# RMS norms of a decoder layer: mean square by float32r products with a constant matrix, inverse root by Ln, Exp and one Newton step

## The chip, the core and the metric

The kernel runs on one core of one Trainium2 chip. The core has five engines that run side by side, each working through its own instructions in order: TensorE (PE) for matrix products, VectorE (DVE) for elementwise work, ScalarE (ACT) for activations and casts, GpSimd (POOL) and SyncE (SP), which here mostly issues the transfers (DMAs) between memory and SBUF. Products land in PSUM, eight banks of 128 x 512 float32. The metric is the device time of one execution in microseconds.

## The reference

One hybrid decoder layer on 1024 tokens of width 1024, float32: a SwiGLU half step (FFN1), a mixer of three branches (RWKV-7, sliding-window attention, cross-attention into 256 memory tokens) merged by gates and one output projection, and a second SwiGLU half step (FFN2). Each of the three has an RMS norm on its input and one on its output, which is then added to the residual stream; the memory tokens have a norm of their own.

```python
def rms_norm(x, g):
    xf = x.astype(jnp.float32)
    y = xf * lax.rsqrt(jnp.mean(xf * xf, axis=-1, keepdims=True) + NORM_EPS)
    return (y * g.astype(jnp.float32)).astype(x.dtype)

f1 = swiglu(rms_norm(h, ffn1_pre_g[l]), ffn1_w_in[l], ffn1_w_out[l])
h = h + HALF_STEP * rms_norm(f1, ffn1_post_g[l])
u = rms_norm(h, mix_pre_g[l])
...
h = h + rms_norm(merged @ w_out[l], mix_post_g[l])
f2 = swiglu(rms_norm(h, ffn2_pre_g[l]), ffn2_w_in[l], ffn2_w_out[l])
h = h + HALF_STEP * rms_norm(f2, ffn2_post_g[l])
```

## The kernel before

**Layout.** Features lie on the partitions and tokens along the free axis: an activation is eight tiles (`KD`) of 128 features by 512 tokens for each of the two halves of the tokens (`HALVES`). A norm thus sums over the partitions and over the eight tiles, and its result, one number for each token, is wanted on all partitions.

**Products.** Every large product is made from three float32r matmuls (`mm3`, lines 330 to 332): an operand is split into a high part, rounded to float32r by ACT, and a low part, the rest, by DVE (`operand`, lines 264 and 266, for weights; `split`, lines 393 and 394, for activations). Weights come as strips into five raw buffers and are split ahead of their use into eight operand buffers (`prefetch`). The two FFN products are computed by a scheme that replaces eight block products by seven and forms sums and differences of blocks on DVE (`factors_part`, `factors_end`, `out_sums`, `out_forms`, `ffn_out_sum`). In an FFN, the first 9 (FFN1) or 13 (FFN2) gates are computed from the first half's factors while the second half's are still being made.

**A norm.** ACT squares the eight tiles and DVE adds them up into one tile `sq` (`sum_squares`, lines 403 and 407; the squares have three buffers of a ring in the pool of the stage). `rstd` does the rest. For each block of 128 tokens, `sq` is the stationary operand of a float32 matmul and a column of ones the moving one, which puts the sum of a token on one partition: `ps_ms`, 128 x 4 for 512 tokens (line 365). On that small tile DVE makes the mean (line 370), a first guess of the inverse root by an integer shift, and three Newton steps (lines 375 to 381). The norms of the layer's last output (`quick`) take a reciprocal on DVE, Sqrt on ACT (line 373) and one Newton step instead. Then four more float32 matmuls, with the column of a block repeated as the stationary operand and the identity as the moving one, spread the result over all partitions: `ps_rs`, 128 x 512 in PSUM (line 387). A float32 matmul stands in the profile as two instructions. The scaling of the eight tiles by gain and root is one DVE instruction each (lines 419, 447 and 730), reading `ps_rs`.

**Where the norms stand.** `factors_norm` normalizes the input of FFN1 (half 0 in `start`, half 1 in `ffn_in`) and of FFN2 (halves 0 and 1); `post_norm` normalizes the output of FFN1, of the mixer's projection and of FFN2, adds the residual (line 733) and, at the end, stores the result; `pre_norm` normalizes the mixer's input. The last output's second half is done in two parts of 256 tokens (`TAIL`). The memory norm calls `rstd` for its columns. With the memory norm there are fourteen.

**Order.** The order of the instructions on each engine is set by a planner, which simulates the engines and takes what is ready, by priority; `high_priority` moves work ahead, and `keep_in_program_order` pins an instruction behind the one traced before it on its engine. Where a norm gets a `between`, its matmuls are pinned, and the function is traced between the two groups of matmuls, so that PE works on other products while the root is made: at the start (`while_x`), and in the last output's norms, where a part of the last product (`more`, `ffn_out`) stands there. Elsewhere the planner places them.

**ACT's tables.** Ln, Exp, Silu, Tanh, Sqrt and Sin each need a table on ACT, and a load (`ACT_TABLE_LOAD`) stands in front of an instruction whose function isn't in the table that is loaded.

Of the kernel before, what the change touches and what calls it, by code (L numbers as in the profile page):

```python
# [24 lines left out]
MEM = 256  # L25
EPS = 1e-6
# [72 lines left out]
class WindowBlock(Block):  # L99
# [108 lines left out]
class Builder:  # L208
# [146 lines left out]

    def rstd(self, sqs, width, pool, n=TH, columns=False, quick=False, between=None):
        nc = self.nc
        V = nc.vector  # L360
        nb = n // P
        ps = self.psum("ps_ms")
        for j in range(nb):
            for i, sq in enumerate(sqs):
                mm = nc.tensor.matmul(ps[:, j : j + 1], sq[:, j * P : (j + 1) * P], self.ones, start=i == 0, stop=i == len(sqs) - 1)
                if between:
                    self.tc.keep_in_program_order(mm)
        m, y, hm, q = (pool.tile([P, 4], F32, tag="rs" + t, name="rs" + t, bufs=2)[:, :nb] for t in "myhq")
        with self.tc.high_priority(offset=self.lead):
            V.tensor_scalar(m, ps[:, :nb], 1.0 / width, EPS, ALU.mult, ALU.add)  # L370
            if quick:
                V.reciprocal(y, m)
                nc.scalar.activation(y, y, ACT.Sqrt)
            else:
                V.tensor_scalar(y.bitcast(I32), m.bitcast(I32), 1, None, ALU.logical_shift_right)
                V.tensor_scalar(y.bitcast(I32), y.bitcast(I32), -1, 0x5F3759DF, ALU.mult, ALU.add)
            V.tensor_scalar(hm, m, -0.5, None, ALU.mult)
            for _ in range(1 if quick else 3):
                V.tensor_tensor(q, y, y, ALU.mult)
                V.tensor_tensor(q, q, hm, ALU.mult)  # L380
                V.scalar_tensor_tensor(y, q, 1.5, y, ALU.add, ALU.mult)
        if between:
            between()
        out = self.psum("ps_rs")
        with self.tc.high_priority(offset=self.lead):
            for j in range(nb):
                mm = nc.tensor.matmul(out[:, j * P : (j + 1) * P], y[:, j : j + 1].broadcast_to([P, P]), self.ident, start=True, stop=True)
                if between:
                    self.tc.keep_in_program_order(mm)
        return (out, y) if columns else out  # L390

    def split(self, x, hi, lo):
        self.nc.scalar.copy(hi, x)  # L393
# [2 lines left out]
    def sum_squares(self, xs, pool):  # L396

        nc = self.nc
        n = xs[0].shape[1]
        acc = None  # L400
        for x in xs:
            sq = pool.tile([P, n], F32, tag=f"sq{n}", name="sq", bufs=3)
            nc.scalar.activation(sq, x, ACT.Square)
            if acc is None:
                acc = sq
            else:
                nc.vector.tensor_tensor(acc, acc, sq, ALU.add)
        return acc

    def pre_norm(self, x, part, gname, u, pool):  # L410

        h, lo, hi = part
        xs = [t[h][:, lo:hi] for t in x]
        rs = self.rstd([self.sum_squares(xs, pool)], D, pool, hi - lo)[:, : hi - lo]
        for k in range(KD):
            if lo == 0:
                u[k][h] = self.u_tile(), self.u_tile()
            t = pool.tile([P, TH], F32, tag="un", name="un", bufs=2)[:, : hi - lo]
            self.nc.vector.scalar_tensor_tensor(t, xs[k], self.vec(gname, k), rs, ALU.mult, ALU.mult)
            self.split(t, *(y[:, lo:hi] for y in u[k][h]))  # L420
# [20 lines left out]
    def factors_norm(self, xs, part, gname, pool, between=None, then=None):  # L441

        h, lo, hi = part
        xs = [x[h][:, lo:hi] for x in xs]
        rs = self.rstd([self.sum_squares(xs, pool)], D, pool, hi - lo, between=between)[:, : hi - lo]
        for k in range(KD) if then else (0, 4, 1, 5, 2, 6, 3, 7):
            self.nc.vector.scalar_tensor_tensor(xs[k], xs[k], self.vec(gname, k), rs, ALU.mult, ALU.mult)
            if then:
                then(k)
# [269 lines left out]
    def post_norm(self, acc, part, gcol, xr, pool, save=None):  # L719

        nc = self.nc
        h, lo, hi = part
        cols = slice(h * TH + lo, h * TH + hi)
        xs = [acc[k][h][:, lo:hi] for k in range(KD)]
        end = save is self.io["out"]
        with self.tc.high_priority(offset=self.urgent if end else 0):
            sq = self.sum_squares(xs[KH:] + xs[:KH] if h else xs, pool)
        rs = self.rstd([sq], D, pool, hi - lo, quick=end, between=self.between if end else None)[:, : hi - lo]
        for k in range(KD):
            nc.vector.scalar_tensor_tensor(xs[k], xs[k], gcol(k), rs, ALU.mult, ALU.mult)  # L730

            e = nc.gpsimd if end and cols.stop == T and k in (0, 2, 4) else nc.vector
            e.tensor_tensor(xs[k], xs[k], xr[k], ALU.add)
            if save is not None:
                nc.sync.dma_start(save[:, k, cols], xs[k])
# [451 lines left out]
    def start(self, x, pool, km_d, vm_d):  # L1187
        nc, tc, io = self.nc, self.tc, self.io
        V = nc.vector
        keep = tc.keep_in_program_order  # L1190
        send = self.send = lambda *a: keep(nc.sync.dma_start(*a))
        mm = lambda *a, start, stop: keep(nc.tensor.matmul(*a, start=start, stop=stop))
# [64 lines left out]
        sqs = mem_squares()  # L1257
# [19 lines left out]
        for i in (0, 1):  # L1277
            t = pool.tile([P, 512], F32, tag="mkv", name="vm", bufs=3)
# [249 lines left out]
    def build(self):  # L1528
        nc, tc, io = self.nc, self.tc, self.io
        with contextlib.ExitStack() as outer, tc.tile_pool(reuse_waits="tile", name="consts", bufs=1) as cp, \  # L1530
# [27 lines left out]
            with quarters() as self.qpool:  # L1558
                x = self.acc_tiles()
# [110 lines left out]
```

## Time and profile before

| | |
|---|---|
| median of 3 runs | 2318.09 us (2318.04 to 2320.25) |
| profiled execution | 2322.86 us, span 2321.1 us |
| PE busy | 2278.9 us, 98% of the span |
| DVE busy | 1653.6 us, 71% |
| ACT busy | 962.3 us, 41% |
| POOL busy | 95.7 us, 4% |
| granted TensorE clock, mean | 0.997 |

The span runs from the first to the last instruction; the profiled execution's own time is 1.8 us longer. A matmul row's duration overlaps with the next one's, so that what a matmul costs PE is read from the starts of its neighbours, not from its duration. Rows of a timeline give start, length, engine, line, operation, output and inputs, shapes and count; in brackets stands the idle time before it and who ended it. PEld is a weight load.

### The profile page before, as it was taken

The numbers are of one execution on the slowest core, as the hardware profiler recorded it, in microseconds if no ns is written. First come the engines' busy times: TensorE is split into PE (matmuls) and PEld (weight loads), VectorE is DVE, ScalarE is ACT, GpSimd is POOL, SyncE is SP. The second block draws the span as 40 slices with busy tenths as digits, with TensorE's granted clock in tenths as the row PEclk, the third lists the DMA queues.
The fourth block names the chain that finished last, engine by engine and source line by source line (L and its number), as shares of the span: only waits on it lengthen the run. The fifth ranks groups of instructions, "written<-read, shape, count | busy, mean of one in ns | idle before, by whom it ended". The sixth has DMA issues, their size and how long they took to land. (4 is left out here: it accounts for less than half of the span.)

```text
span 2321.1 us, 33883 instructions
## 1 busy us (share of the span) xinstructions
PE 2278.9 (98%) x12080; PEld 1862.7 (80%) x12080; DVE 1653.6 (71%) x2790; ACT 962.3 (41%) x1791; POOL 95.7 (4%) x134
## 2 busy tenths in 40 slices
PE   8999999999999999999999999999999999999998
PEld 6778888888888777888878888778888778888887
DVE  6998666666688786895645466565899886666666
ACT  5522333454445544223444455234552223345451
POOL 0000000000000000001310000241000000000000
PEclk9999999999999999999999999999999999999999
DMA  8577545586644446325435425555467775558663
GB/s 276 160 251 255 171 158 166 171 289 207 190 160 144 111 118 186 131 96 183 139 130 179 129 95 170 173 178 160 158 212 229 263 243 172 168 182 271 214 195 114
DMA packets 280778, 417.70 MB, mean 180 GB/s; under 512 B 82304, under 2 KB 104320, under 8 KB 280352
## 3 DMA queue, kind: packets, MB, share of 16 engines
q1 hardware_dynamic: 231552, 388.20, 51.9%
q10 hardware_dynamic: 49056, 27.34, 4.2%
q8 instruction: 95, 1.56, 0.3%
q14 instruction: 75, 0.61, 0.1%
HBM read 284.89 MB, written 129.50 MB: 179 GB/s over the span
## 5 line engine op out<-in xcount | busy, mean ns | idle before, releaser
L264 ACT CAST w_hi<-w_raw 128x512 fp32r<-128x512 f32 x594 | 366.2, 620 | 774.8 <-PE px L331 140.9
L266 DVE TENSOR_TENSOR w_lo<-w_raw,w_hi 128x512 fp32r<-128x512 f32 x594 | 415.4, 702 | 218.0 <-ACT w_hi L264 181.1
L330 PE MATMUL po<-u,w_hi 128*128 128x512 f32 (+1 forms) x476 | 181.8, 382 | 0.0
L332 PE MATMUL po<-u,w_lo 128*128 128x512 f32 (+1 forms) x476 | 181.1, 380 | 0.0
L331 PE MATMUL po<-u,w_hi 128*128 128x512 f32 (+1 forms) x476 | 181.0, 380 | 0.0
L330 PE MATMUL pgate<-u,w_hi 128*128 128x512 f32 x384 | 155.2, 404 | 0.0
L332 PE MATMUL pgate<-u,w_lo 128*128 128x512 f32 x384 | 151.5, 394 | 0.0
L331 PE MATMUL pgate<-u,w_hi 128*128 128x512 f32 x384 | 149.7, 390 | 0.0
L330 PE MATMUL px<-f,w_hi 128*128 128x512 f32 x352 | 139.0, 395 | 6.4 <-DVE up L600 3.9
L330 PE MATMUL px<-u,w_hi 128*128 128x512 f32 x352 | 137.5, 391 | 3.0 <-ACT w_hi L264 2.1
L331 PE MATMUL pz<-u,w_hi 128*128 128x512 f32 x352 | 137.3, 390 | 0.6 <-DVE u L394 0.6
L331 PE MATMUL px<-f,w_hi 128*128 128x512 f32 x352 | 137.6, 391 | 0.0
L330 PE MATMUL pz<-u,w_hi 128*128 128x512 f32 x352 | 137.3, 390 | 0.3 <-DVE m L587 0.3
L332 PE MATMUL px<-f,w_lo 128*128 128x512 f32 x352 | 137.5, 391 | 0.0
L331 PE MATMUL px<-u,w_hi 128*128 128x512 f32 x352 | 137.0, 389 | 0.0
L332 PE MATMUL pz<-u,w_lo 128*128 128x512 f32 x352 | 137.0, 389 | 0.0
L332 PE MATMUL px<-u,w_lo 128*128 128x512 f32 x352 | 137.0, 389 | 0.0
L394 DVE TENSOR_TENSOR u<-hid,u 128x512 fp32r<-128x512 f32 x114 | 78.5, 689 | 49.2 <-ACT u L393 46.6
L331 PEld LDWEIGHTS po<-u,w_hi 128*128 128x128 f32 x476 | 89.5, 188 | 17.3
L332 PEld LDWEIGHTS po<-u,w_lo 128*128 128x128 f32 x476 | 89.5, 188 | 17.3
L330 PEld LDWEIGHTS po<-u,w_hi 128*128 128x128 f32 x476 | 89.5, 188 | 17.2
L393 ACT CAST u<-hid 128x512 fp32r<-128x512 f32 x114 | 70.7, 620 | 69.6 <-DMA hid<-form_d 61.8
(347 smaller groups left out, 5127.6 us busy)
## 6 DMA issues: line engine op xcount, KB each, us to landing
w_raw<-in_ffn_in SPq DMA_DIRECT2D x220, 256.0 KB
hid<-form_d SPq DMA_DIRECT2D x154, 256.0 KB
w_raw<-in_win SPq DMA_DIRECT2D x112, 256.0 KB
ws<-in_ffn_out SPq DMA_DIRECT2D x88, 256.0 KB
form_d<-g SPq DMA_DIRECT2D x88, 256.0 KB
ffn_sum_d<-ws SPq DMA_DIRECT2D x88, 256.0 KB
w_raw<-ffn_sum_d SPq DMA_DIRECT2D x88, 256.0 KB
form_d<-h SPq DMA_DIRECT2D x66, 256.0 KB
```

Source lines behind the costliest of these rows:

```text
L264: self.nc.scalar.copy(hi, x)
L266: self.nc.vector.tensor_tensor(lo, x, hi.bitcast(F32), ALU.subtract)
L330: mm(out, wh, xh, start=first, stop=False, **kw)
L331: mm(out, wh, xl, start=False, stop=False, **kw)
L332: mm(out, wl, xh, start=False, stop=last, **kw)
L393: self.nc.scalar.copy(hi, x)
L394: self.nc.vector.tensor_tensor(lo, x, hi.bitcast(F32), ALU.subtract)
```

## The change

All norms but the memory norm take a new function, `inverse_root`. ACT copies the sum of squares, with a small constant added that stands for epsilon, into a float32r tile (`sq_hi`), and DVE makes the rest (`sq_lo`). Two float32r matmuls with a constant 128 x 128 matrix of 1/1024 as the stationary operand put the mean on all partitions, 128 x 512 in PSUM. ACT takes Ln of it, then Exp with a scale of -0.5, and squares that; two DVE instructions make one Newton step over the full width. The result lies in SBUF; the scalings read it there. The table that has both Ln and Exp is asked for right behind the high part. All ACT instructions of the function but none of DVE's are pinned in the traced order, the two matmuls only where there is a `between`; the function `between` is traced behind all of it. The high part, the low part and the root share the ring of the squares, which has four buffers in place of three. Two constant tiles are set at the start. `rstd` keeps one form, for the memory norm.

```diff
-    def rstd(self, sqs, width, pool, n=TH, columns=False, quick=False, between=None):
+    def rstd(self, sqs, width, pool, n, between):
...
-            if quick:
-                V.reciprocal(y, m)
-                nc.scalar.activation(y, y, ACT.Sqrt)
...
+    def inverse_root(self, sq, pool, between=None):
+
+        nc = self.nc
+        n = sq.shape[1]
+        hi, lo, y = (pool.tile([P, n], t, tag=f"sq{n}", name=name, bufs=4) for t, name in ((F32R, "sq_hi"), (F32R, "sq_lo"), (F32, "rs")))
+        ps = self.psum("ps_rs")[:, :n]
+        V, S = nc.vector, nc.scalar
+        keep = self.tc.keep_in_program_order
+        with self.tc.high_priority(offset=self.lead):
+            keep(S.activation(hi, sq, ACT.Identity, bias=self.eps))
+            V.scalar_tensor_tensor(lo, sq, self.eps, hi.bitcast(F32), ALU.add, ALU.subtract)
+            keep(S.preload_act_table_set("natural_log_exp_and_others"))
+            for i, x in enumerate((hi, lo)):
+                mm = nc.tensor.matmul(ps, self.mean_r, x, start=i == 0, stop=i == 1)
+                if between:
+                    keep(mm)
+            keep(S.activation(y, ps, ACT.Ln))
+            keep(S.activation(y, y, ACT.Exp, scale=-0.5))
+            keep(S.activation(sq, y, ACT.Square))
+            V.scalar_tensor_tensor(sq, ps, -0.5, sq, ALU.mult, ALU.mult)
+            V.scalar_tensor_tensor(y, sq, 1.5, y, ALU.add, ALU.mult)
+        if between:
+            between()
+        return y
...
-            sq = pool.tile([P, n], F32, tag=f"sq{n}", name="sq", bufs=3)
+            sq = pool.tile([P, n], F32, tag=f"sq{n}", name="sq", bufs=4)
...
-        rs = self.rstd([self.sum_squares(xs, pool)], D, pool, hi - lo)[:, : hi - lo]
+        rs = self.inverse_root(self.sum_squares(xs, pool), pool)
...
-        rs = self.rstd([self.sum_squares(xs, pool)], D, pool, hi - lo, between=between)[:, : hi - lo]
+        rs = self.inverse_root(self.sum_squares(xs, pool), pool, between)
...
-        rs = self.rstd([sq], D, pool, hi - lo, quick=end, between=self.between if end else None)[:, : hi - lo]
+        rs = self.inverse_root(sq, pool, self.between if end else None)
...
-        ps, col = self.rstd(sqs, D, pool, MEM, True, between=while_mem)
+        ps, col = self.rstd(sqs, D, pool, MEM, while_mem)
...
+            self.mean_r = cp.tile([P, P], F32R, name="mean_r")
+            nc.vector.memset(self.mean_r.bitcast(F32), 1.0 / D)
+            self.eps = cp.tile([P, 1], F32, name="eps")
+            nc.vector.memset(self.eps, EPS * D / P)
```

More of the change, by code (lines that the diff above doesn't have):

```diff
@@ L364, in rstd @@
             for i, sq in enumerate(sqs):
-                mm = nc.tensor.matmul(ps[:, j : j + 1], sq[:, j * P : (j + 1) * P], self.ones, start=i == 0, stop=i == len(sqs) - 1)
-                if between:
-                    self.tc.keep_in_program_order(mm)
+                keep(nc.tensor.matmul(ps[:, j : j + 1], sq[:, j * P : (j + 1) * P], self.ones, start=i == 0, stop=i == len(sqs) - 1))
         m, y, hm, q = (pool.tile([P, 4], F32, tag="rs" + t, name="rs" + t, bufs=2)[:, :nb] for t in "myhq")
@@ L381, in rstd @@
                 V.scalar_tensor_tensor(y, q, 1.5, y, ALU.add, ALU.mult)
-        if between:
-            between()
+        between()
         out = self.psum("ps_rs")
@@ L386, in rstd @@
             for j in range(nb):
-                mm = nc.tensor.matmul(out[:, j * P : (j + 1) * P], y[:, j : j + 1].broadcast_to([P, P]), self.ident, start=True, stop=True)
-                if between:
-                    self.tc.keep_in_program_order(mm)
-        return (out, y) if columns else out
+                keep(nc.tensor.matmul(out[:, j * P : (j + 1) * P], y[:, j : j + 1].broadcast_to([P, P]), self.ident, start=True, stop=True))
+        return out, y
+    def inverse_root(self, sq, pool, between=None):
[4 more added lines that the diff above has]
+        V, S = nc.vector, nc.scalar
+        keep = self.tc.keep_in_program_order
+        with self.tc.high_priority(offset=self.lead):
[4 more added lines that the diff above has]
+                mm = nc.tensor.matmul(ps, self.mean_r, x, start=i == 0, stop=i == 1)
+                if between:
+                    keep(mm)
[5 more added lines that the diff above has]
+        if between:
+            between()
+        return y
     def split(self, x, hi, lo):
```

7 lines of the change are left out of this document (3 added, 4 removed).

## The prediction

> **What bounds the kernel now.** I read the page first (engines and slices), then the table by stage, the groups by line, and the timeline at each norm. The columns of the stage rows are the stretch, its length, then busy time of PE, weight loads, DVE, ACT and POOL, granted clock, DMA share, GB/s.
>
> ```profile
> PE 2278.9 (98%) x12080; PEld 1862.7 (80%) x12080; DVE 1653.6 (71%) x2790; ACT 962.3 (41%) x1791; POOL 95.7 (4%) x134
> ...
> 40.00:100.00 60.00, 57.37 (x255) 45.90 (x254) 50.07 (x93) 33.56 (x59) 0.00 (x0) 1.00 0.58 188
> 1700.00:1900.00 200.00, 195.47 (x853) 158.25 (x852) 182.38 (x299) 65.71 (x116) 0.00 (x0) 1.00 0.72 237
> ...
> 1805.07 0.47 PE L330 MATMUL px<-f,w_hi 128*128 128x512 f32 x1 [1.37 <-DVE up L600]
> ```
>
> PE has 98% of the span, so a PE slot given back is time given back, except where another engine sets the pace. That is so behind the norms of the second token half in both FFNs: DVE is busy 182.38 of 200 us from 1700 on, and PE waits for DVE (1.37 us at 1805.07). In such a stretch a shorter PE only waits longer. ACT has room.
>
> **Terms.** Thirteen norms change (the memory norm keeps its path). By place: A (25 us) and B (60) ahead of FFN1; C, D (640, 671) post and pre norm of half 0, E, F (694, 722) of half 1 behind FFN1; G, H (1616, 1641) and I, J (1668, 1697) the same around the mixer's output; K (2252), L (2296), M (2310) at the end. L and M have 256 columns, the rest 512.
>
> *PE.* The groups and one norm (H) in the timeline, where a weight load or matmul of another line follows at once:
>
> ```profile
> L365 PE MATMUL ps_ms<-ones,sq x96: 164/250/271, 24.6 to 2310.7; 128*128 128x1 f32 x96
> L387 PE MATMUL ps_rs<-ident,rsy x100: 270/275/376, 28.9 to 2312.7; 128*128 128x128 f32 x100
> ...
> 1639.60 1.48 DVE L407 TENSOR_TENSOR sq<-sq 128x512 f32<-128x512 f32 x2
> 1641.23 1.02 PE L365 MATMUL ps_ms<-ones,sq 128*128 128x1 f32 x8 [0.40 <-DVE sq L407]
> 1642.12 0.48 PE L332 MATMUL pw<-u,w_lo 128*128 128x512 f32 x1
> 1642.43 0.40 PE L330 MATMUL pw<-u,w_hi 128*128 128x512 f32 x1
> 1643.12 0.39 PE L330 MATMUL pw<-u,w_hi 128*128 128x512 f32 x1
> 1643.29 0.16 DVE L381 SCALAR_TENSOR_TENSOR rsy<-rsq,rsy 128x4 f32<-128x4 f32 x1
> 1643.49 0.16 DVE L379 TENSOR_TENSOR rsq<-rsy 128x4 f32<-128x4 f32 x1
> 1644.94 1.05 PE L387 MATMUL ps_rs<-ident,rsy 128*128 128x128 f32 x8
> 1645.75 0.48 PE L332 MATMUL pw<-u,w_lo 128*128 128x512 f32 x1
> 1646.03 1.41 DVE L447 SCALAR_TENSOR_TENSOR acc<-acc,vecs,ps_rs 128x512 f32<-128x512 f32 x2 [0.23 <-PE ps_rs L387]
> ```
>
> The 96 matmuls are 11 norms of 8 and 2 of 4; of the other 100, 4 are the memory norm's and stay. At H the means hold PE from 1641.23 to 1642.12 (0.89 us) and the spread from 1644.94 to 1645.75 (0.81); the next matmul after each then comes some 0.1 us late (1642.12 to 1642.43 against 0.23, from 1642.43 to 1643.12 in three). That is 1.9 us a norm. The two float32r products are of the kind that runs here each 0.23 us: 0.46. Saved: 1.4 us at 512 columns, by halves 0.7 at 256; at most 11 x 1.4 + 2 x 0.7 = 16.8 us.
>
> *The chain from the last sum of squares to the first scaling.* At H it takes 1646.03 - (1639.60 + 1.48) = 4.95 us. Thirteen small DVE steps at 0.20 us (1643.29 to 1643.49) are 2.6 us of DVE in it. The new steps:
>
> ```profile
> L403 ACT ACTIVATE sq<-acc 128x512 f32<-128x512 f32 x88 | 54.3, 630 | 27.4 <-DVE acc L733 9.7 <-DVE acc L685 8.0 <-DVE sq L407 7.8
> L403 ACT ACTIVATE sq<-acc 128x256 f32<-128x256 f32 x16 | 6.6, 417 | 30.8 <-DVE acc L685 28.6 <-DVE sq L407 1.2 <-DVE rsm L370 0.9
> L1119 ACT ACTIVATE yrs<-var,gn_eps 128x512 f32<-128x512 f32 x8 | 5.5, 684 | 5.4 <-PE var L1117 5.4
> L730 DVE SCALAR_TENSOR_TENSOR acc<-acc,post,ps_rs 128x512 f32<-128x512 f32 x24 | 17.0, 741 | 1.5 <-PE ps_rs L387 1.5
> L730 DVE SCALAR_TENSOR_TENSOR acc<-acc,post,ps_rs 128x256 f32<-128x256 f32 x16 | 7.0, 471 | 0.9 <-PE ps_rs L387 0.9
> ...
> L264 ACT CAST w_hi<-w_raw 128x512 fp32r<-128x512 f32 x594 | 366.2, 620 | 774.8 <-PE px L331 140.9
> ...
> 51.61 0.62 ACT L403 ACTIVATE sq<-acc 128x512 f32<-128x512 f32 x1
> 52.25 1.28 ACT L566 ACT_TABLE_LOAD   x1
> 53.55 0.63 ACT L566 ACTIVATE g<-g 128x512 f32<-128x512 f32 x1
> ```
>
> Rounding to the high part 0.68 (the row with a bias), the low part on DVE 0.74, product 0.40, Ln 0.65, Exp and Square 0.63 each, two Newton steps 0.74 each, is 5.21; with some 0.03 from a step to the next that depends on it (1643.29 + 0.16 to 1643.49) and 0.1 to 0.15 onto another engine, 5.6 us. So 0.6 longer than H, but other norms take longer than H, since the small steps queue between DVE's other work. I put the chain down as unchanged where other work fills PE, bounds -1 to +1 us each. DVE's work stays: 2.6 us out, 3 x 0.74 = 2.2 in. ACT gains 2.6 us a norm, 33 in all, beside 962 busy of 2321. Behind a Ln that waits for PE stand the casts of the weights; they are ahead of their use, since they idle 774.8 us, mostly until PE gives a buffer back (row L264), so a delay of a few us is hidden there.
>
> *Tables.* Ln and Exp need a table, the FFN's Silu another: where Silu runs around a norm (B, I, J) it is a switch there and one back. A load costs 1.30 us here (52.25 to 53.55), and nothing more, since the Square before it ended at 52.23. The load stands behind the high part, beside 0.74 + 0.40 us of DVE and PE: nearly covered. The Trainium skill, page "ScalarE: Activation LUTs", section "What ACT_TABLE_LOAD costs", puts a further drain of about 1380 ns on each switch, 2.66 us in all. The trace has no such gap; by the page the load would outlast its cover by some 1.4 us in each chain.
>
> *Waits on PE.* The second product now waits for the high and low parts, 0.1 + 0.68 + 0.03 + 0.74 + 0.15 = 1.7 us after the sum, with the next projection's matmuls behind it in PE's order. For K and L, whose products are pinned, there is room:
>
> ```profile
> 2247.24 0.68 DVE L407 TENSOR_TENSOR sq<-sq 128x512 f32<-128x512 f32 x1
> 2251.77 0.95 PE L365 MATMUL ps_ms<-ones,sq 128*128 128x1 f32 x8
> ...
> 2293.09 0.42 DVE L407 TENSOR_TENSOR sq<-sq 128x256 f32<-128x256 f32 x1 [0.54 <-ACT sq L403]
> 2295.76 0.54 PEld L365 LDWEIGHTS ps_ms<-ones,sq 128*128 128x128 f32 x4
> ...
> 693.26 0.69 DVE L407 TENSOR_TENSOR sq<-sq 128x512 f32<-128x512 f32 x1
> 695.37 0.73 DVE L419 SCALAR_TENSOR_TENSOR un<-acc,vecs,ps_rs 128x512 f32<-128x512 f32 x1
> ...
> 737.16 0.39 PE L332 MATMUL pq<-u,w_lo 128*128 128x512 f32 x1
> 738.62 1.29 DVE L394 TENSOR_TENSOR u<-un,u 128x512 fp32r<-128x512 f32 x2
> ...
> 2309.80 0.43 DVE L407 TENSOR_TENSOR sq<-sq 128x256 f32<-128x256 f32 x1 [0.54 <-ACT sq L403]
> 2310.38 0.58 PE L365 MATMUL ps_ms<-ones,sq 128*128 128x1 f32 x4 [1.58 <-DVE sq L407]
> 2312.32 0.68 PE L387 MATMUL ps_rs<-ident,rsy 128*128 128x128 f32 x4 [1.36 <-DVE rsy L381]
> 2313.04 1.26 DVE L730 SCALAR_TENSOR_TENSOR acc<-acc,post,ps_rs 128x256 f32<-128x256 f32 x3 [0.87 <-PE ps_rs L387]
> ```
>
> K's sum is ready 3.9 us, L's 2.2 us ahead. C to H aren't pinned: the planner places the products, and can put them where the parts are ready; I take no wait, bounds 0 to 1.7 us each.
>
> *Buffers.* High part, low part and root share one ring of four with the squares, and the root is held through eight scalings, where before it lay in PSUM. At E the sum ends at 693.95 while D's last scaling starts at 695.37: if a square of E gets D's root buffer, E is late by up to 1.4 us and the squares behind it (five of 0.7), 4.9 us in all. I take nothing, since three other buffers are free by then. The freed PSUM bank, the two memsets at the start and the unchanged DMAs cost and give nothing: no queue is passed.
>
> *M.* Nothing covers it. Now: 2313.04 - 2310.23 = 2.81 us. New: 0.10 + 0.47 (Square's 0.417 and the bias) + 0.02 + 0.47 + 0.15 + 0.30 (two products of 256 columns, the first under the low part) + 0.05 + 0.42 + 0.03 + 0.42 + 0.03 + 0.42 + 0.02 + 2 x 0.50 = 3.9 us, +1.1; a table load that isn't dropped, though its table is in place, adds 0.3.
>
> *Sum.* A and B: 0, since B's factors come off a DVE-paced stretch, and A's earlier start runs into B's (bounds -3 to +4). C, D: -2.8. E, F: -1.2. PE comes to half 1's projections at 737.4 (737.16 + 0.23) and to their eighth block 21 matmuls, 4.8 us, later at 742.2; that block's low part is ready at 739.91, so 2.3 us of an earlier PE can count, less 1.1 for two chains longer by 0.6 (bounds -2.8 to 0). G, H: -2.8, PE-bound. I, J: 0, DVE-paced (-2.8 to +2). K, L: -1.4 - 0.7 = -2.1. M: +1.1. Together -7.8 us. The profiled execution took 2322.86 us (span 2321.1), 4.8 above the median 2318.09; taken off the median, that is 2310.3, 2310 as the forecast. Within 0.2% (4.6 us, about what a measurement tells from nothing) lies 2313.5 to 2322.7.
>
> **Rivals.**
> (1) Every PE slot counts: -16.8 - 0.6 (waits like H's 0.40, before the products) + 1.1 = -16.3, 2301.8. For it: 98% PE everywhere, even 195.47 of 200 in the DVE-paced stretch. Against: the 1.37 us waits there.
> (2) PE waits for the split: half to all of 1.7 us at C to H, +5.1 to +10.2 on the forecast: 2315.4 to 2320.5, no change to be measured. For it: H's means already waited 0.40 us for the sum. Against: the planner knows both parts' times.
> (3) Slower: Silu gets between load, Ln and Exp at B, I and J. Precedent, in the chain of waits (start, length, what): a gate's table load (L1153) stands between the group norm's Ln and its Exp (L1123).
>
> ```profile
> 1198.36 1.27 ACT L1153
> 1200.84 0.97 ACT yrs L1123
> ```
>
> In one gap it costs two switches, 2.6 + 0.6 of longer chain = 3.2 each, 9.6 in three: 2319.9, still no change. In both gaps 5.2 + 0.6 = 5.8, three times 17.4: 2327.7. It decides from 4.1 us a chain. By the page's 2.66 us the same would be 11.2 each and 2344; nothing in the trace bears that.
> (4) The change gives PE nothing: the planner moves other work into worse places, 2319 (M's 1.1 left).
>
> **How the numbers follow.** Forecast (2304 to 2313.5) 0.46, rival 1 (below 2304) 0.17, rival 2 (with rival 3 in one gap) 0.19, rival 3 in both gaps 0.15, rival 4 0.03. The time is the forecast's. The range 2301 to 2322 leaves out rival 3 and the edge of rival 1, 0.2 together. Faster is the forecast and rival 1, 0.63; the same is rivals 2 and 4, 0.22; slower is rival 3, 0.15.
>
> **What would show it.** Right: 8 means' and 8 spread matmuls replaced by 2 of 0.23 us; PE busy down by some 17 us; the first scaling in M some 3.9 us after the sum; from 1700 on more PE idle, released by DVE, than now. The low part at C to H without PE idle before the product. Wrong: PE idle ahead of these products (rival 2), more than one table load there and one back at B, I or J (rival 3), or PE idle from 1700 on no longer than now (rival 1).

## The result, and the profile after

The changed kernel takes 2357.69 us (median of 4, 2356.57 to 2365.87) against 2319.17 us (2318.04 to 2322.82) before: ratio 1.0172, 95% interval 1.0157 to 1.0186. It is slower by 38.5 us, outside the range, on the side that had a chance of 0.15. The profiled execution of after took 2365.87 us, 8 more than the median, so differences of spans below are a little larger than those of medians.

The page after: busy time by engine.

```profile
PE 2316.3 (98%) x11914; PEld 1852.2 (78%) x11914; DVE 1658.5 (70%) x2683; ACT 1008.4 (43%) x1856; POOL 93.9 (4%) x134
```

PE runs 166 matmuls fewer than before (12080), as it should: 192 out, 26 in. Yet it is busy 37.4 us longer (2278.9 before). Of the 43.1 us by which the span is longer (2364.2 against 2321.1), only 5.7 are more idle time of PE; the rest is the same work taking longer. Where? A stretch inside FFN1, in which no norm stands, 200 to 400 us, as the table by stage shows it (length, busy time and count of PE, weight loads, DVE, ACT, POOL, then granted clock, DMA share, GB/s). First before, then after:

```profile
200.00:400.00 200.00, 200.00 (x884) 165.57 (x883) 139.27 (x225) 71.44 (x122) 0.00 (x0) 1.00 0.51 170
```

```profile
200.00:400.00 200.00, 200.00 (x859) 161.04 (x858) 133.56 (x215) 69.15 (x117) 0.00 (x0) 1.00 0.49 165
```

PE never idles in either, the granted clock is 1.00 in both, and after gets through 25 matmuls fewer. The timeline of PE shows the pitch; before, then after, each from one matmul to the ninth behind it:

```profile
300.12 0.39 PE L330 MATMUL px<-f,w_hi 128*128 128x512 f32 x1
...
302.16 0.39 PE L330 MATMUL px<-u,w_hi 128*128 128x512 f32 x1
```

```profile
300.02 0.40 PE L330 MATMUL pz<-u,w_hi 128*128 128x512 f32 x1
...
302.12 0.40 PE L330 MATMUL px<-f,w_hi 128*128 128x512 f32 x1
```

2.04 us against 2.10 us for nine, 227 against 233 ns each; this time from start to start is called the pitch below. Over the whole traces, its mean over neighbouring 512-column matmuls of lines 330 to 332 is 227.2 ns in 8078 of them before, and 233.3 ns in 7856 of them after. 6.1 ns times 7856 is 48 us. This is code that the diff doesn't touch. Not all of it reaches the end, as e1 below shows, which has this pitch and no other change: it is 28.8 us behind before at 1552 us, still 29.0 at 1955 us, behind the stretch that DVE paces, and 37.6 at 2331 us.

The parts that the change does touch look as announced. The groups by line of after, for the two products (durations min/median/max, then what ended the idle time before them), and then PE's timeline of after at H:

```profile
L397 PE MATMUL ps_rs<-sq_hi,mean_r x13: 279/498/583, 24.5 to 2351.4; 128*128 128x512 f32 x11, 128*128 128x256 f32 x2
...
L397 PE MATMUL ps_rs<-sq_lo,mean_r x13: 280/454/496, 25.0 to 2351.9; 128*128 128x512 f32 x11, 128*128 128x256 f32 x2
...
  ACT sq_hi L393: 9.6, 13
  DVE sq_lo L394: 2.8, 9
```

```profile
1668.35 0.40 PE L332 MATMUL pw<-u,w_lo 128*128 128x512 f32 x1
1668.66 0.51 PE L397 MATMUL ps_rs<-sq_hi,mean_r 128*128 128x512 f32 x1
1669.00 0.40 PE L330 MATMUL pw<-u,w_hi 128*128 128x512 f32 x1
...
1669.46 0.48 PE L397 MATMUL ps_rs<-sq_lo,mean_r 128*128 128x512 f32 x1
1669.78 0.39 PE L332 MATMUL pw<-u,w_lo 128*128 128x512 f32 x1
```

Two matmuls a norm, with projection matmuls between them while DVE makes the low part. PE waited 9.6 us for the high part and 2.8 us for the low one over all 13 norms (the two rows that name who ended the idle time).

### The profile page after: what moved, and what is told of

It reads as the page before. It is cut to its first block, busy times and chain, and to the rows that moved or that the text cites. A ratio compares the mean times of both kernels' runs of the same rounds, so it can differ in the third digit from the quotient of the medians.

```text
span 2364.2 us, 33492 instructions
## 1 busy us (share of the span) xinstructions
PE 2316.3 (98%) x11914; PEld 1852.2 (78%) x11914; DVE 1658.5 (70%) x2683; ACT 1008.4 (43%) x1856; POOL 93.9 (4%) x134
## 5 line engine op out<-in xcount | busy, mean ns | idle before, releaser
L332 PE MATMUL pgate<-u,w_lo 128*128 128x512 f32 x384 | 153.3, 399 | 0.0
L330 PE MATMUL px<-f,w_hi 128*128 128x512 f32 x352 | 141.9, 403 | 10.2 <-DVE u L604 8.7
L331 PE MATMUL px<-f,w_hi 128*128 128x512 f32 x352 | 140.9, 401 | 0.3 <-DVE f L411 0.2
L331 PEld LDWEIGHTS po<-u,w_hi 128*128 128x128 f32 x476 | 89.5, 188 | 19.7
L330 PEld LDWEIGHTS po<-u,w_hi 128*128 128x128 f32 x476 | 89.5, 188 | 19.7
```

Of the source, the lines that this page charges most:

```text
L330: mm(out, wh, xh, start=first, stop=False, **kw)
L331: mm(out, wh, xl, start=False, stop=False, **kw)
L332: mm(out, wl, xh, start=False, stop=last, **kw)
```

## The experiments

### Where the tiles lie

The pools are laid out one behind another from each end of SBUF. The new constants, `mean_r` (512 bytes per partition) and `eps` (4 bytes, which take 32), stand ahead of the weights' buffers and move them up by 544 bytes; the activations' buffers hang at the other end and don't move. In the compiled programs, which list every tile's address, the weights (`w_hi`, `w_lo`) of nearly all large products start 224 bytes past a multiple of 512 before and 256 after; the activations (`u`) start at 480 in both. Before, 192 matmuls of FFN1's output product (`form`, 504 to 688 us) read other activations, 32 bytes off the weights modulo 256; those already took 233.7 ns. So theory one: the pitch depends on the addresses of the two operands relative to each other. Rival: on something else that the change moved (the planner's order, the DMAs, the table loads).

**e1**: the kernel before, with a constant tile of 32 bytes that nothing reads. No norm is changed.

```diff
             nc.vector.memset(self.ones, 1.0)
+            self.pad = cp.tile([P, 1], F32, name="pad")
+            nc.vector.memset(self.pad, 0.0)
```

> The kernel before with one more constant tile of 128 x 1 (32 bytes a partition), set and never read, which moves the weight operands and all that lies above them by 32 bytes, while the activation operands of the pool on the other side stay. Theory (place in SBUF): a float32r product whose two operands don't lie at the same offset within 64 bytes takes 233 ns instead of 227 ns from start to start; about 8080 products change to that, +0.0063 us each, +51 us: 2369 us. Rival (the work of the change, its order and its chains make the loss): the time stays at 2318 us.

**e2**: the same tile in the changed kernel.

> The changed kernel with one more such tile, so that its constants move the rest by 576 bytes in place of 544. Theory (place, 64 bytes): weights at 288, activations at 480 of 512, 192 apart, a multiple of 64; 7860 products go back to 227 ns, -50 us: 2308 us. If 256 bytes are what counts, they stay at 233 ns and the time at 2357 us. Rival (the work): 2357 us.

**e3**: the changed kernel, with `eps` in one more column of the tile of gains, whose slot has room for it. What stands ahead of the weights grows by exactly 512 bytes.

```diff
-            self.vecs = cp.tile([P, NVEC], F32, name="vecs")
-            nc.scalar.dma_start(self.vecs, io["vecs"])
+            self.vecs = cp.tile([P, NVEC + 1], F32, name="vecs")
+            nc.scalar.dma_start(self.vecs[:, :NVEC], io["vecs"])
...
-            self.eps = cp.tile([P, 1], F32, name="eps")
+            self.eps = self.vecs[:, NVEC:]
```

> The changed kernel with epsilon in a spare column of the vectors' tile, so that the constants move the rest by 512 bytes exactly: the same offsets within 512 bytes as before. Theory (place): 227 ns, 2308 us, and what is left of the difference to 2318 us is what the norms give. Rival (the work): 2357 us.

**e4**: e1, and a tile of 32 bytes that nothing reads at the other end of SBUF, ahead of the activations.

```diff
+            right = outer.enter_context(tc.tile_pool(reuse_waits="tile", name="right", bufs=1, side="right"))
+            nc.vector.memset(right.tile([P, 1], F32, name="rpad"), 0.0)
             self.upool = outer.enter_context(tc.tile_pool(reuse_waits="tile", name="u", bufs=32, side="right"))
```

> The kernel before with 32 bytes more on both sides: weights at 256, activations at 448 of 512. Theory (the offset of one operand against the other): they stay 192 apart, 227 ns, 2318 us. Rival theory (the place of each by itself: multiples of 64 bytes are the slow ones): 233 ns, 2369 us. Rival (the work): 2318 us, which only e1 tells from the first.

**e5**: e1 with 128 bytes in place of 32.

> The kernel before with one unused constant tile of 128 bytes per partition, so that nearly all factor products read weights at 352 and activations at 480 bytes past a multiple of 512, 128 apart. If the slow pitch is there whenever the two operands differ modulo 256 bytes: 233 ns from product to product and 2359 to 2362 us, as with 32 bytes. If only the last 128 bytes of the address count: 227 ns and 2316 to 2321 us. If the cost grows with the distance of the two (32 apart one way was 6 ns): more than 233 ns and over 2365 us.

**e6**: e4 with 224 bytes on the left in place of 32.

> The kernel before with 224 bytes of unused constant on the left side of SBUF and 32 bytes on the right side: weights move up to 448, activations move down to 448 bytes past a multiple of 512, so both are moved and their distance modulo 256 is 0 again (modulo 512 it is 0 where before had 256). If only the distance modulo 256 counts: 227 ns and 2316 to 2321 us. If what counts is that either operand has left the place that it had before, or that the two must lie in different halves of 512 bytes: 233 ns and 2358 to 2362 us.

Measured; the addresses are those of the operands of most matmuls, modulo 512, and the pitch is the mean start-to-start time of those of them that have a neighbour:

| kernel | weights | activations | distance mod 256 | pitch, ns (count) | median, us | ratio to before (95%) |
|---|---|---|---|---|---|---|
| before | 224 | 480 | 0 | 227.2 (8078) | 2319.17 beside after, 2322.38 beside e1 to e4, 2321.80 beside e5 and e6 | 1 |
| after | 256 | 480 | 224 | 233.3 (7856) | 2357.69 | 1.0172 (1.0157 to 1.0186) |
| e1 | 256 | 480 | 224 | 233.3 (7871) | 2360.99 | 1.0167 (1.0152 to 1.0182) |
| e2 | 288 | 480 | 192 | 233.3 (7863) | 2361.63 | 1.0168 (1.0153 to 1.0183) |
| e3 | 224 | 480 | 0 | 227.1 (7850) | 2321.15 | 1.0001 (0.9991 to 1.0012) |
| e4 | 256 | 448 | 192 | 233.3 (7867) | 2361.17 | 1.0176 (1.0159 to 1.0193) |
| e5 | 352 | 480 | 128 | 232.7 (7874) | 2355.78 | 1.0147 (1.0133 to 1.0161) |
| e6 | 448 | 448 | 0 | 227.1 (8041) | 2321.33 | 1.0001 (0.9991 to 1.0010) |

The stretch from 200 to 400 us again, in e1, e3 and e6:

```profile
200.00:400.00 200.00, 199.89 (x857) 160.67 (x856) 133.65 (x216) 69.71 (x118) 0.00 (x0) 1.00 0.50 164
```

```profile
200.00:400.00 200.00, 199.97 (x882) 165.26 (x881) 137.81 (x223) 71.47 (x121) 0.00 (x0) 1.00 0.51 169
```

```profile
200.00:400.00 200.00, 200.00 (x884) 165.64 (x884) 139.11 (x225) 71.55 (x122) 0.00 (x0) 1.00 0.51 170
```

e1 shows that 32 unused bytes cost the old kernel what the change costs (8 us less than the 2369 us written down, since the stretch that DVE paces takes up a part), and e3 that the change without the shift costs nothing, though it doesn't reach the 2308 us either. The rival falls. What is left is the form of the rule:

- e2 was to return to the fast pitch if 64 bytes were the unit, as I had put it. It didn't: 192 apart is a multiple of 64.
- The text for e4 counts wrongly. Before, the two are 256 apart (480 - 224). Tiles at the right end move down, so e4's are 192 apart (448 - 256), and the "relative" theory, rightly applied, says slow. Slow it was; the miss is the text's, and e4 alone decides nothing.
- e5 excludes 128 as the unit. Its pitch is a little below that at 32, 192 and 224, and its time 3 us below the 2359 us expected at least.
- e6 is the test that e4 was meant to be: both operands moved, equal modulo 256, equal even modulo 512, where before they differ by 256. Fast, as expected of the distance alone. Since 448 is a multiple of 64, e6 also rules out the other theory of e4's text, that each operand's own place counts.

In every run here, with small groups of matmuls at other addresses too (activations at 0, 96 or 192 beside weights 256 higher: 227.0 to 228.3 ns; 32 bytes apart: 233.1 to 233.7 ns), the fast pitch goes with a distance of 0 modulo 256. Distances of 32, 128, 192 and 224 are slow; others weren't tried. In these runs only the relation between the two operands matters, not the place of either.

The Trainium skill, page "SBUF — State Buffer", section "Who interferes with whom", gives TensorE two read ports, one for the moving operand and one for the weight load, and calls them independent; nothing there depends on addresses. The runs differ from that: moving the weights alone changes the time (e1), so do activations 32 bytes off beside the same weights (233.7 ns in the kernel before), and moving both by the right amounts changes it back (e6). What happens inside isn't shown.

### What became of the norms' own gain

e3 is the change without the shift, and it gains nothing (1.0001). Compared matmul by matmul, in start times, it runs 1.9 us ahead of before behind A and B, 6.4 us at 726 us (behind C to F), 6.5 us at 1618 us (G) and 11.0 us at 1716 us (behind I's and J's products), and by 1824 us only 2.2 us. Between the last two PE waits. After itself shows the same (PE's timeline):

```profile
1773.01 0.80 PE L330 MATMUL px<-f,w_hi 128*128 128x512 f32 x1 [8.01 <-DVE u L604]
```

```profile
1740.11 0.79 PE L330 MATMUL px<-f,w_hi 128*128 128x512 f32 x1 [8.30 <-DVE u L604]
```

The second is e3's. Why is DVE late there? J in after, rows of DVE's timeline and of ACT's in one order:

```profile
1726.96 1.48 DVE L424 TENSOR_TENSOR sq<-sq 128x512 f32<-128x512 f32 x2
...
1729.61 1.28 ACT L395 ACT_TABLE_LOAD   x1
1731.03 0.60 ACT L400 ACTIVATE rs<-ps_rs 128x512 f32<-128x512 f32 x1
...
1732.03 0.64 ACT L401 ACTIVATE rs<-rs 128x512 f32<-128x512 f32 x1
1732.68 1.28 ACT L583 ACT_TABLE_LOAD   x1
1733.97 0.63 ACT L583 ACTIVATE g<-g 128x512 f32<-128x512 f32 x1
...
1734.98 0.63 ACT L402 ACTIVATE sq<-rs 128x512 f32<-128x512 f32 x1
...
1738.05 4.71 DVE L464 SCALAR_TENSOR_TENSOR acc<-acc,vecs,rs 128x512 f32<-128x512 f32 x7
```

A Silu of FFN2 (L583), with its table load, stands between Exp (L401) and Square (L402): 1732.67 to 1734.98, 2.3 us. From the end of the sum (1728.44) to the first scaling it is 9.61 us, at I 10.28, where before took 5.90 and 5.35:

```profile
1666.50 1.48 DVE L407 TENSOR_TENSOR sq<-sq 128x512 f32<-128x512 f32 x2
...
1673.33 1.41 DVE L730 SCALAR_TENSOR_TENSOR acc<-acc,vecs,ps_rs 128x512 f32<-128x512 f32 x2 [0.15 <-PE ps_rs L387]
...
1695.68 0.69 DVE L407 TENSOR_TENSOR sq<-sq 128x512 f32<-128x512 f32 x1
...
1702.27 2.06 DVE L447 SCALAR_TENSOR_TENSOR acc<-acc,vecs,ps_rs 128x512 f32<-128x512 f32 x3 [0.25 <-PE ps_rs L387]
```

Theory: the length of these two chains sets when DVE comes to the splits that FFN2 reads next, and so PE's wait. Rival: PE is merely early for a DVE that would pace this stretch anyway. All the following runs have e3's layout.

**e7**: the square of the Newton step on DVE, at all norms.

```diff
-            keep(S.activation(sq, y, ACT.Square))
+            V.tensor_tensor(sq, y, y, ALU.mult)
```

> The change with its small constant put into the last column of the vector of gains (the layout of before), and the square of the Newton step as a product on DVE instead of on ACT. In the run without this edit a Silu and its table load stood between Exp and Square at I and J, sum to first scaling was 10.2 and 9.45 us, and PE then waited 8.30 us at 1740 us for a split of DVE. If that third gap is what the two chains pay: nothing can get in behind Exp, each chain is 2.3 to 3.0 us shorter, the wait at 1740 falls to between 2.5 and 4.5 us and the time to 2315 to 2318 us. If the Silu only moves into another gap of the chain (ahead of Ln or of Exp) or the added DVE work takes the place of it: chains still over 9 us, 2320 to 2323 us.

2310.43 us (2308.59 to 2312.53), ratio 0.9952 (0.9939 to 0.9964). At I and J the chain is 6.5 and 6.1 us, and PE's wait 3.82 us. The mechanism is as expected; the time is 5 us better than expected. Of the 9.8 us by which PE is ahead of e3 at the last matmul, 4.5 are that wait.

Some 3 us more come from a place that the expectation left out: B has the third gap too. In e3, Exp starts there at 59.15 us, then come a load and a Silu, and Square starts at 62.10. From the sum to the first scaling it is 10.2 us in after, e3 and e11, 6.5 in e7 and 6.3 before. Behind it PE waits for the split in e3, and not in e7:

```profile
93.10 0.50 PE L331 MATMUL px<-u,w_hi 128*128 128x512 f32 x1 [0.81 <-DVE u L411]
95.56 0.50 PE L330 MATMUL px<-u,w_hi 128*128 128x512 f32 x1 [0.80 <-ACT u L410]
```

At 125 us e7, e9 and e12, which all have the square on DVE, are 3.1, 2.8 and 2.9 us ahead of e3; e8 and e11, which have it on ACT at B, are 0.8 behind and 0.5 ahead.

**e8**: the old `rstd` at I and J alone; at M no table load, and the root written to PSUM.

```diff
+        if save is self.h2 and h:
+            rs = self.rstd([sq], D, pool, hi - lo)[:, : hi - lo]
+        else:
+            rs = self.inverse_root(sq, pool, self.between if end else None, end and cols.stop == T)
...
-            keep(S.preload_act_table_set("natural_log_exp_and_others"))
+            if not last:
+                keep(S.preload_act_table_set("natural_log_exp_and_others"))
...
+            out = ps if last else y
-            V.scalar_tensor_tensor(y, sq, 1.5, y, ALU.add, ALU.mult)
+            V.scalar_tensor_tensor(out, sq, 1.5, y, ALU.add, ALU.mult)
```

> The change in the layout of before, but the norms I and J (second half behind the mixer) with the root of the kernel before, and the last norm M without its own table load and with the root written to PSUM, from which the eight scalings read it. If the length of the chains at I and J is what made PE wait 8.30 us at 1740 us: that wait is gone or under 1 us, 7 to 9 us stay saved up to 2301 us. At M the load of 1.28 us is gone and first scaling to last addition takes 5.0 us rather than 6.5. Together 2308 to 2312 us. If instead PE simply came too early for a DVE that paces this stretch anyway, PE waits 5 to 8 us at the same place with the old chains too, and the time is 2316 to 2319 us. If the scalings at the end are slow for POOL beside them and not for the place of the root, they still take 6.5 us.

2313.15 us (2309.00 to 2314.32), ratio 0.9958 (0.9945 to 0.9970): 1 us above the upper end expected, the rival's time not reached. PE's wait is 1.03 us, with chains of 6.31 and 5.40 us; PE is 12.7 us ahead of before at 1714 us and still 12.9 ahead at 1813 us. So the chains' length it was.

**e11**: the DVE square at I and J alone.

> The change in the layout of before, the Newton square on DVE at I and J alone, on ACT at the eleven others. If what the square on ACT cost was the Silu with its table load between Exp and Square at I and J, this keeps most of the 10.7 us that the DVE square brought at all norms: PE's wait at 1740 us falls from 8.30 to under 4.5 us and the time is 2311 to 2316 us. If the gain came in parts from all norms: the wait stays over 6 us or the time over 2317 us. Nothing is expected before 1640 us: 3.0 us at A and B and 3.2 us around 1571 us, which the DVE square at all norms had gained, should be missing if they belong to the edit, and be there if they are run-to-run drift.

2319.89 us (2314.68 to 2323.71), ratio 0.9996 (0.9987 to 1.0005). By its numbers this is the other branch of the expectation, for a reason that it didn't have: PE's wait is 8.55 us. The edit did what it should at I (6.50 us), but at J the planner now put the Silu elsewhere (ACT's timeline):

```profile
1690.31 1.28 ACT L395 ACT_TABLE_LOAD   x1
1691.60 1.28 ACT L586 ACT_TABLE_LOAD   x1
1692.89 0.63 ACT L586 ACTIVATE g<-g 128x512 f32<-128x512 f32 x1
...
1694.02 1.28 ACT L400 ACT_TABLE_LOAD   x1
1695.32 0.60 ACT L400 ACTIVATE rs<-ps_rs 128x512 f32<-128x512 f32 x1
...
1696.44 1.28 ACT L401 ACT_TABLE_LOAD   x1
1697.73 0.63 ACT L401 ACTIVATE rs<-rs 128x512 f32<-128x512 f32 x1
```

The load of the Ln and Exp table is followed at once by Silu's (L586, the line that was 583). Ln then needs another load and Exp a third. The chain at J is 11.74 us. Put in order, over all these runs:

| kernel | chain at I, us | chain at J, us | PE's wait behind them, us |
|---|---|---|---|
| before | 5.35 | 5.90 | none |
| e8 | 6.31 | 5.40 | 1.03 |
| e7 | 6.51 | 6.10 | 3.82 |
| e3 | 10.2 | 9.45 | 8.30 |
| after | 10.28 | 9.61 | 8.01 |
| e11 | 6.50 | 11.74 | 8.55 |

e11 has I's chain short and J's long, and its wait is that of both long. That doesn't make J's the one that decides: the two stand one behind the other on DVE. From I's first scaling to J's sum it takes 22.5 to 23.1 us in every kernel of the table, so a longer I makes J as much later. The two chains together are 11.7 us in e8, 12.6 in e7, 18.2 in e11, 19.7 in e3 and 19.9 in after. From J's first scaling to the end of PE's wait it takes 38.0, 37.5, 35.5, 34.3 and 35.0 us in the same order, so some 3 us of a late start are made up. The rows behind the table's last column, from e8, e7 and e11:

```profile
1731.17 0.50 PE L330 MATMUL px<-f,w_hi 128*128 128x512 f32 x1 [1.03 <-DVE u L618]
```

```profile
1730.91 0.50 PE L330 MATMUL px<-f,w_hi 128*128 128x512 f32 x1 [3.82 <-DVE u L604]
```

```profile
1736.59 0.79 PE L330 MATMUL px<-f,w_hi 128*128 128x512 f32 x1 [8.55 <-DVE u L607]
```

e7 and e8 get to the end of the wait at the same time (1730.91, 1731.17): e7 arrives 3.1 us earlier and waits 2.8 us longer. That much of the rival is true: what PE gains by then is not kept.

A long wait also costs more than its length. The next 4 us behind it as the table by stage shows them, e8, then e3:

```profile
1731.10:1735.10 4.00, 3.93 (x17) 3.28 (x18) 3.11 (x6) 0.00 (x0) 0.00 (x0) 1.00 0.58 171
```

```profile
1740.10:1744.10 4.00, 3.99 (x10) 3.18 (x11) 2.45 (x5) 0.00 (x0) 0.00 (x0) 0.53 0.57 186
```

The granted clock is 1.00 in e8 and about half in e3, which gets through 10 matmuls where e8 gets through 17. In the seven kernels in which PE waits 3.8 us or more at this place (after, e2, e3, e7, e9, e11, e12), the clock is at 0.5 for 3.4 to 10.2 us around the end of the wait (1737.0 to 1743.9 us in e3); in the other six, with 1.03 us (e8) or none, it stays at 1.00. So e3's lead falls by 10.3 us there, with a wait of 8.3. That the wait is the reason for the clock was not tested.

e11 was also to show whether e7's lead at A, B and G is the edit's. It is ahead of e3 by 2 us at 241 us and by 3.9 us at 1614 us, though the two programs have the same instructions in the same order on PE, ACT and DVE up to I. Of the first, 1.6 us come between 145 and 154 us, where e3's clock is at 0.5 for 3.4 us (149.8 to 153.3) and e11's is not; at 125 us it is 0.5 us. Of the second, 1.7 us come between 1540 and 1571 us, where e7, e8, e9, e11 and e12 all gain 1.4 to 1.7 us on e3, whatever their edit. e3 also has a stretch of half clock from 1518.6 to 1522.0 that e7, e8 and e12 have not; they gain 1.1 to 1.4 us around it. So the lead at B is the edit's, and what e7 gains around G comes from this one execution of e3.

### The end

In e3 (as in after) the tail gives back what is left. M in after: the chain, then the first row of the scalings, the last addition:

```profile
2350.35 0.42 DVE L424 TENSOR_TENSOR sq<-sq 128x256 f32<-128x256 f32 x1 [0.54 <-ACT sq L420]
...
2351.34 1.28 ACT L395 ACT_TABLE_LOAD   x1
...
2354.86 1.75 DVE L747 SCALAR_TENSOR_TENSOR acc<-acc,post,rs 128x256 f32<-128x256 f32 x3
2355.56 0.76 POOL L750 TENSOR_TENSOR acc<-acc,x_re 128x256 f32<-128x256 f32 x1 [749.70 <-DVE acc L747]
...
2360.95 0.43 DVE L750 TENSOR_TENSOR acc<-acc,x_re 128x256 f32<-128x256 f32 x1
```

4.09 us from the sum to the first scaling, 6.52 us from there to the end of the last addition (2361.38). Before, the second was 5.03 us (2313.04 to 2318.07). The first three scalings take 1.75 us, not 1.26, beside an addition on POOL. Two readings: POOL beside a DVE that now takes both tensors from SBUF, or the root in SBUF by itself.

**e9**: e7, and at M no table load, and the root in PSUM (the last two edits of e8).

> The change in the layout of before, the Newton square on DVE at all norms, and at the last norm M no table load of its own and the root written to PSUM. The two edits touch different places, so their gains should add: up to 2296 us as with the DVE square alone (span 2310.8 us there), then 1.28 us less in the chain of M minus at most 0.3 that the products need anyway, and 1.3 to 1.5 us less from first scaling to last addition: 2306.5 to 2309 us. If the load at M only covered a wait for the products, or the scalings at the end are paced by POOL's three additions, there is nothing at the end: 2310 to 2312 us.

**e12**: e7, with POOL's three additions at the end on DVE.

```diff
-            e = nc.gpsimd if end and cols.stop == T and k in (0, 2, 4) else nc.vector
-            e.tensor_tensor(xs[k], xs[k], xr[k], ALU.add)
+            nc.vector.tensor_tensor(xs[k], xs[k], xr[k], ALU.add)
```

> As with the Newton square on DVE at all norms, but the three additions of POOL at the last norm are DVE's, so POOL does nothing beside the eight scalings; the root is still read from SBUF. If a scaling is slow because POOL works beside it (978 ns at most, against 472 to 480 alone): all of the sixteen of 256 columns take 470 to 500 ns. If the reading of a root from SBUF is slow by itself at this place: still some near 900 ns. First scaling to last addition would be eight scalings and eight additions on one engine, 6.5 to 7.2 us, so the time is the same or up to 1 us longer.

e9: 2310.52 us (2306.83 to 2311.30), ratio 0.9952 (0.9938 to 0.9965), not to be told from e7. e12: 2308.54 us, a single run. The scalings of 256 columns are the shorter form in these groups (min/median/max ns); e7, e9 and e12:

```profile
L747 DVE SCALAR_TENSOR_TENSOR acc<-acc,post,rs x40: 472/744/978, 634.9 to 2307.1; 128x512 f32<-128x512 f32 x24, 128x256 f32<-128x256 f32 x16
```

```profile
L749 DVE SCALAR_TENSOR_TENSOR acc<-acc,post,ps_rs x8: 468/472/481, 2300.6 to 2304.8; 128x256 f32<-128x256 f32 x8
```

```profile
L747 DVE SCALAR_TENSOR_TENSOR acc<-acc,post,rs x40: 477/745/752, 633.0 to 2302.6; 128x512 f32<-128x512 f32 x24, 128x256 f32<-128x256 f32 x16
```

With the root in SBUF and POOL at work a scaling takes up to 978 ns; with the root in PSUM (e9) or POOL idle (e12) none of 256 columns is slow. Both conditions are needed. The Trainium skill states just that ("SBUF — State Buffer", "Who interferes with whom"): a DVE instruction with two SBUF inputs contends with a GpSimd instruction that reads SBUF, since its second input comes through a read port that the two share, and one with at most one SBUF input doesn't. From first scaling to last addition e9 takes 5.13 us as expected. e12 takes 5.94 us, less than the 6.5 to 7.2 that I had put down.

The other half of e9's expectation failed. Without its table load M's chain is 4.05 us (2296.57 to 2300.62), against 4.10 with it in e7: the load lay beside the low part and the products. In e8 against e3, both with the square on ACT, it is 3.84 against 4.08. There M's products take 0.38 us each, in e9 and e7 0.58, so that in e9 the products end about when the load would have. The load is worth 0.05 to 0.25 us, not 1.

## Why the prediction was wrong, and where it was right

**The step that failed** is the sentence under buffers: "The freed PSUM bank, the two memsets at the start and the unchanged DMAs cost and give nothing: no queue is passed." The setting of the two tiles costs nothing that shows, but the room they take does: 32 of their 544 bytes take the weights out of step with the activations, and 6.1 ns on each of nearly 8000 matmuls follow. e1 is that step alone: 38.6 us on the median. None of the rivals contained it, and none of them came near 2358 us.

**I, J: 0, bounds -2.8 to +2.** The forecast that a shorter PE only waits longer in the DVE-paced stretch is right. But the bound above was too low: e3's PE was 7.8 us ahead before I and 11.0 behind J's products, and kept 2.2. Rival 3 had the mechanism and the three places, B, I and J, but two gaps, between load and Ln and between Ln and Exp. The one that opened in after at all three is the third, between Exp and Square, which I had left out since Square needs no table of its own. The loads are as many as forecast (one there and one back at each of the three), but the one back stands inside the chain. The chains got longer by 3.9 us at B, 4.9 at I and 3.7 at J, near the 4.1 us a chain from which that rival was to decide, and with the gap went the whole gain of the norms: e7, which closes it, has it. e11 then showed the first gap of rival 3, between load and Ln, at a higher price: 5.84 us more than before at J where one gap was put at 3.2, since the loads that follow Silu hold Ln and Exp apart, so that Exp needs one too.

**The chain elsewhere, 5.6 us, "unchanged", ±1.** At H it is 6.85 us after (1674.64 - 1667.79) against 4.95. The sum of the steps left out what ACT runs between them, a cast, a copy and another cast of some 0.5 us each ahead of Ln, Exp and Square:

```profile
1669.92 0.62 ACT L264 CAST w_hi<-w_raw 128x512 fp32r<-128x512 f32 x1
1670.45 0.59 ACT L400 ACTIVATE rs<-ps_rs 128x512 f32<-128x512 f32 x1
1670.94 0.58 ACT L1542 COPY acc<-pw 128x512 f32<-128x512 f32 x1
1671.40 0.64 ACT L401 ACTIVATE rs<-rs 128x512 f32<-128x512 f32 x1
```

DVE's small steps had queued too, but there were no such neighbours on an engine of which the prediction said that it has room.

**PE's slot, 1.9 to 0.46 us, 1.4 saved.** Measured at H 0.66 us (1668.66 to 1669.00 and 1669.46 to 1669.78) and 0.08 of wait: 1.2 saved. **C to F** brought 4.6 us in e3 (1.9 to 6.4) and 5.2 in e7 against the 4.0 forecast, but that the sum is near is luck: C and D brought 1.2 us in e3 instead of 2.8, since PE waits at C, and E and F 3.4 instead of 1.2, since the deduction there was too large. G and H brought 3.0 in e3, against 2.8. A and B, put at 0, show 1.9 us in e3, inside the bounds, and 3.8 in e7, 0.8 outside them, since the gap at B is closed there. That the buffers' ring costs nothing isn't contradicted by any row. **Rival 2** holds at one norm of six. In PE's timeline, from the matmul before the high part's product to that product, less one pitch of 0.23 us, C has 0.97 us after and 1.88 in e3, D to H at most 0.14 after and 0.48 in e3; ahead of the low part's product PE never waits at C to H. Together some 3 us in e3, of which before had 1.2 ahead of its means; the rival needed 5.1 to 10.2 more.

**Tables.** A switch cost 1.28 to 1.30 us with nothing behind it, in after as before (load at 1732.68, Silu at 1733.97), so the further 1380 ns that the Trainium skill, page "ScalarE: Activation LUTs", section "What ACT_TABLE_LOAD costs", puts on a switch are not seen here either. That the load is "nearly covered" holds at M (e8, e9).

**M, +1.1.** 4.09 us against the 3.9 forecast, or 4.2 with its load: right. Missing is what came behind it: the scalings with the root in SBUF beside POOL, 1.5 us. The tail from PE's last matmul to the end is 2.5 us longer in e3 than before, 1.3 in e9.

Without the shift, the forecast of 2310 would have been met by e7 (2310.43, from -11.4 us against the before of the same chip), and the change as written would have taken as long as before (1.0001), inside the range but without a gain.

## What to carry to other kernels

A tile that nothing reads can cost more than the work that a change saves: when constants or buffers are added, compare the pitch of matmuls in a stretch that the change doesn't touch, and if it moved at the same clock, compare the addresses of weights and moving operand modulo 256. When a chain is moved from DVE to ACT, list every place between its steps where the planner may put work with another table, and keep the steps on ACT next to one another; a gap in front of a step that needs no table counts too. A wait of TensorE can cost more than its length, so look at the granted clock behind it. Of two tensors that DVE reads beside work of POOL, one was better held in PSUM here.

## What the runs showed of the hardware that I had not expected

- A float32r matmul of 512 columns follows the one before it after 227 ns if its weights and its moving operand start at equal addresses modulo 256 bytes, and after 233 ns at distances of 32, 192 and 224 (232.7 at 128), at the same granted clock; eight kernels, some 7850 to 8080 matmuls in each. Whether it is so for other types and widths was not tried.
- A DVE scaling of 256 columns with both tensors in SBUF takes up to 978 ns instead of 472 beside POOL's additions, and 468 to 481 with one of them in PSUM.
- Around the end of PE's waits of 3.8 to 8.6 us behind J the granted clock is at 0.5 for 3.4 to 10.2 us, in seven kernels of seven; with 1.03 us or none, never there.
- With the same instructions, the lead of one profiled execution over another drifts by up to 4 us on the way (e3 against e11 ahead of I), 1.6 us of it at a single stretch of half clock, so a gain of a few us is to be read next to its cause.
